# Six column chunks of the merge gates as seven-for-eight block products, moved behind the recurrent branch

## The chip, the cores and the metric

The kernel runs on one core of one Trainium2 chip. The metric is the device time in microseconds (us) of one execution, median of three runs. The engines are named as in the profile: PE multiplies matrices (PEld is its weight load), DVE, ACT and POOL work on tiles, SP issues most of the transfers.

## What is computed

One trunk layer of a streaming encoder, 512 frames by 1024 features, in float32. Cut to what the change touches:

```python
xn = rmsnorm(x, norm_mix_g)
q, k, v, xr, gr, ga, gb = split(xn @ w_in)      # seven parts of 1024 columns each
ya = chunked_band_attention(q, k, v) @ w_attn_out
xc = causal_depthwise_conv(xr)                  # four taps
r, i = sigmoid(block_diag(xc, w_rg_r) + b_r), sigmoid(block_diag(xc, w_rg_i) + b_i)
a = exp(-8 * r * softplus(-lam))
h = scan(a, sqrt(1 - a * a) * i * xc)           # h[t] = a[t] * h[t-1] + ...
yb = (h * gelu(gr)) @ w_rnn_out
out = x + (sigmoid(ga + b) * ya + sigmoid(gb + b) * yb) @ w_o   # then the feed-forward half
```

## The kernel before

**Products.** Every float32 operand is split into a high and a low part (ACT copies the high part, DVE subtracts it to leave the low one: `split`, lines 80 to 83), and every product is three matmuls (`mm3`, lines 74 to 78). A projection of `xn` goes by chunks of 256 columns: `project` makes two output tiles of 128 columns by 512 frames, each with 8 blocks of the contraction times 3 matmuls, so 48 matmuls of 512 frames a chunk. The feed-forward half makes ten pairs of its chunks in another way (`block_product`, line 360): a chunk is cut into 2 by 2 blocks of the weights and 2 by 2 blocks of the activations, and seven products of the blocks' sums stand for the eight products of the blocks. That is 7 times 4 times 3, or 84, matmuls of 256 frames. The sums of the weights' blocks are made by DVE for each chunk (`weight_sums`), those of the activations once.

**Room for weights.** A chunk's raw weights land in one of three `raw` tiles and are split into `whl` tiles, of which there are four, two to a chunk; the list `chunks` says in which order. `weights(name, ahead)` makes the chunk and the next `ahead` ones.

**The stage around the change.** After the norm comes the recurrent branch, in four pairs of feature tiles (j = 0, 2, 4, 6). A pair's work is:

- the chunk `xr`; then `rnn_conv`: ACT `conv_in` (L668), three DVE taps (L675), ACT L679 and POOL L680 split the result into `xch`;
- the chunk `gr`; then the GeLU: ACT L691, DVE L692, ACT L696, DVE L697. It makes a tile `g`, of which there are two, out of a PSUM bank `t`, of which there are two;
- `gates_of`: twelve small matmuls (`rg`, L709) read `xch`; then eight ACT gates (L721), two ACT tiles `u` (L728), two exponentials (L729), DVE L731, POOL L733, DVE L735, L736; one ACT square root for the pair (L759, with a table load before and one behind it); then for each tile `rnn_scan`: DVE L740, the scan L741, L742, which reads `g` for the last time, and ACT L746 and POOL L747 for the two parts of `rnn`;
- one or two chunks of the merge gates `ga`, `gb` with a `tanh` each (L780).

So the order on PE is xr0, gr0, ga0, rg(0), gb0, xr2, gr2, rg(2), ga2, gb2, xr4, gr4, rg(4), gb4, xr6, gr6, rg(6), gb6; then q and k of the first pair of heads, v, the recurrent branch's way out `yb` (contracting over all eight `rnn` tiles), and the attention. The chunks ga4 and ga6 come late in the attention.

**What sets the order.** Apart from marked stretches the order of each engine's instructions is made when the kernel is built, by a scheduler that takes whatever it holds to be ready, in general the earliest in the text first; an instruction far down in the text may so be placed early if its room and its inputs are free. `keep_in_program_order` puts an instruction behind everything of its engine that is ahead of it in the text. On the chip each engine then goes through its list in order.

Of the kernel before, what the change touches and what calls it, by code (L numbers as in the profile page):

```python
# [14 lines left out]
P = 128  # L15
D = 1024
S = 512
# [21 lines left out]
def block_kernel(ctx: ExitStack, tc: tile.TileContext, x, norm_mix_g, w_in, b_merge, rel_table,  # L39
# [31 lines left out]
    def mm_tile(name, tag="mm"):  # L71
        return ps.tile([P, S], F32, tag=tag, bufs=4 if tag == "mm" else 2, name=name)

    def mm3(o, sh, sl, mh, ml, start, stop, parts=False):

        pe.matmul(o, sh, mh, start=start, stop=False, skip_group_check=parts)  # L76
        pe.matmul(o, sh, ml, start=False, stop=False, skip_group_check=parts)  # L77
        pe.matmul(o, sl, mh, start=False, stop=stop, skip_group_check=parts)  # L78
# [14 lines left out]
    index = {}  # L93
    strassen = [f"f{w}{j}" for j in range(2, FT, 2) for w in "gu"]

# [14 lines left out]
    def plan_v(gr):  # L110
        plan(f"v{gr}", cols(w_in, C_V + gr * CW))

    plan_qk(0)
# [43 lines left out]
    def load(name, k):  # L157
        _, parts, rows, kts = chunks[index[name]]
        wide = sum(width for *_, width in parts)
        n = min(4 * CW // wide, kts - k)  # L160
        at = rows + k * P
        pl, bufs = wp, 3
        if name in strassen and name[0] == "f":
# [12 lines left out]
    room = [None]  # L176

    begun = {}
    spare = [None]

    def weight_sums(name, ahead=False):
# [8 lines left out]
        if name not in begun:  # L190
            a11, a21, a12, a22 = blocks_of()
            s21, s34 = (sums_room.tile([P, 2, 4, P], F32, tag=tag, bufs=1, name=f"{tag}_{name}")
                        for tag in ("s21", "s34"))
            s2, s1, s3, s4 = s21[:, 0], s21[:, 1], s34[:, 0], s34[:, 1]
            first_sum = dve.tensor_add(s1, a21, a22)
            if name == "fu2":

                tc.keep_in_program_order(first_sum)
            dve.tensor_sub(s2, s1, a11)
            dve.tensor_sub(s3, a11, a21)  # L200
            dve.tensor_sub(s4, a12, s2)
        if ahead:
            slots[0] += 1
            o = sums_room.tile([P, 2, 2, 4, P], F32R, tag="whl", bufs=1, name=f"whl_{name}_s2")
# [11 lines left out]
        for group in ((("a11", a11), ("a12", a12)), (("s2", s2), ("s1", s1)), (("s3", s3), ("s4", s4)), (("a22", a22),)):  # L216
# [10 lines left out]
            if len(group) == 2:  # L227
                slots[0] += 1
                pl, tag, bufs = (sums_room, "whl", 1) if slots[0] % 5 == 1 else (wp, "whl", 4)
            o = pl.tile([P, len(group), 2, 4, P], F32R, tag=tag, bufs=bufs, name=f"whl_{name}_{group[0][0]}")  # L230
# [236 lines left out]
    gm = cp.tile([P, 8], F32, name="gm")  # L467
    _, xnT = features(xnp, "xn", "xnT")

# [233 lines left out]

    def rnn_gate_products(j, xch, tag):

        pos = [ps.tile([P, S], F32, tag=tag, bufs=4 if tag == "mm" else 2, name=f"rg{j}_{n}") for n in range(2)]
        for n, (wp_, xp) in enumerate(((0, 0), (1, 0), (0, 1))):
            for po, rows in zip(pos, (slice(0, HD), slice(HD, P))):
                ins = pe.matmul(po[:], wrg[rows, wp_, j], xch[rows, xp], start=n == 0, stop=n == 2)  # L709
                if j == n == 0:  # L710

                    tc.keep_in_program_order(ins)
        return pos

# [39 lines left out]
    def gates_of(j):  # L754
        pos = [rnn_gate_products(j + c, conv[j + c][1], ("s", "mm")[c]) for c in range(2)]
        for c in range(2):
# [21 lines left out]
    def gate(w, j):  # L778
        po = tile_of(f"g{'ab'[w]}{j - j % 2}", j % 2, "t" if j < 2 and w == 0 else "mm")
        act.activation((ta, zB)[w][j], po[:], AF.Tanh, bias=hb[:, 16 + 8 * w + j:17 + 8 * w + j], scale=0.5)  # L780
# [4 lines left out]
    with tc.manual_schedule(engines={mybir.EngineType.Activation, mybir.EngineType.DVE}):  # L785
        po = [tile_of("xr0", c, ahead=0) for c in range(2)]
        xc = [conv_in(0, po[0])]
        conv_taps(0, po[0], xc[0])
        prefetch(index["ga0"] + 1)
        xc.append(conv_in(1, po[1]))  # L790
# [5 lines left out]
        g.append(gelu_in(1, po[1]))  # L796
        prefetch(index["gb0"] + 1)
        for c in range(2):
            gelu_out(g[c], po[c])
            conv[c] = xc[c], xch[c], g[c]  # L800
    for j in range(0, KT, 2):
        if j:
            for c in range(2):
                conv[j + c] = rnn_conv(j + c, tile_of(f"xr{j}", c, ahead=2))
        for c in range(2):
            if j:
                po = tile_of(f"gr{j}", c, "t")
                conv[j + c] += (rnn_gelu(j + c, po),)
        if j:
            gates_of(j)  # L810
        for w in range(j // 4, 2):
            for c in range(2):
                gate(w, j + c)
            if j == w == 0:
                gates_of(j)

# [43 lines left out]
    rw2_stack.close()  # L860
    rw_stack.close()
    aw2_stack, aw2 = opened("aw2", 2)
    aw_stack, aw = opened("aw", 2, "right")
# [140 lines left out]

    sums_room = ctx.enter_context(pool_of("sums", 1, "right"))
    hn_stack, hnp = opened("hnT", 1, "right")
# [111 lines left out]
    def split_act(i):  # L1118
        o = act2[i]

        if i == 0:
            hi = acp.tile([P, 2, S], F32R, tag="act", bufs=13, name=f"act_hi{i}")
        elif i < 3:
            hi = sums_room.tile([P, 2, S], F32R, tag=("s21", "s34")[i - 1], bufs=1, name=f"act_hi{i}")
        else:
            if i == 3:
                hi_room.append(sums_room.tile([P, 2, 2, S], F32R, tag="whl", bufs=1, name="act_hi34"))
            hi = hi_room[0][:, i - 3]
# [231 lines left out]
```

## Time and profile before

| what | value |
|---|---|
| median of 3 runs | 867.27 us (867.13 to 867.33) |
| the profiled execution: its own time, its span | 867.3 us, 865.5 us |
| DVE, ACT, POOL busy over the span | 600.9, 498.1, 95.2 us |
| rg(0), rg(2), rg(4), rg(6) start at | 47.5, 82.0, 127.4, 161.8 us |
| first and last matmul of `yb` start at | 191.0, 241.4 us |
| first block product of the feed-forward half starts at | 544.9 us |

The profiled execution is the time of the runs within 0.1 us, so sums made against its span are sums against the median; 1.8 us lie outside the span. A busy time of an engine adds up the intervals in which it had an instruction in work. Matmuls overlap in their pipe, so the time that one takes up on PE is read from the distance of two starts, not from its own duration.

### The profile page before, as it was taken

The page shows a single profiled execution, that of the slowest core. Times are in us where ns is not written, and L with a number is a line of the kernel's source. Part 1 is how long each engine was busy: PE and PEld are TensorE (multiplying, and loading weights), DVE is VectorE, ACT ScalarE, POOL GpSimd, SP SyncE. Part 2 cuts the span into 40 slices and gives each one's busy share as a digit, 9 for nine tenths or more (in the row PEclk, how much of TensorE's full clock was granted, in tenths as well). Part 3 has the DMA queues.
Part 4 walks back from the last instruction along what each step waited for, and adds up shares of the span by engine and source line. Part 5 has one row for each costly group of instructions (what it writes and reads, how often), then busy time and mean ns, then how long its engine had stood idle before and what let it go on. Part 6 is the DMA issues. An engine that isn't in the chain of part 4 may idle for free.

```text
span 865.5 us, 13353 instructions
## 1 busy us (share of the span) xinstructions
PE 856.4 (99%) x5130; PEld 761.1 (88%) x5130; DVE 600.9 (69%) x950; ACT 498.1 (58%) x878; POOL 95.2 (11%) x161
## 2 busy tenths in 40 slices
PE   9999999999999999999999999999999999999997
PEld 6988888888889889898888889999999999888885
DVE  5666656573456585766556556988888888698885
ACT  6595747752356585767633357555555556545434
POOL 2412111120112132221200000000000001000000
PEclk9999999999999999999999999999999999999999
DMA  9133232433323332232223712424333332437542
GB/s 289 57 119 106 68 120 76 123 98 98 109 88 95 81 103 74 81 113 64 74 76 121 266 51 72 145 79 131 109 98 98 99 98 85 148 100 227 185 134 97
DMA packets 88767, 96.39 MB, mean 111 GB/s; under 512 B 5784, under 2 KB 74992, under 8 KB 88704
## 3 DMA queue, kind: packets, MB, share of 16 engines
q1 hardware_dynamic: 87072, 92.03, 34.3%
q10 hardware_dynamic: 1232, 2.95, 0.9%
q8 instruction: 40, 0.66, 0.3%
q0 software_dynamic: 400, 0.57, 0.2%
q14 instruction: 23, 0.19, 0.1%
HBM read 93.39 MB, written 2.14 MB: 110 GB/s over the span
## 4 chain that ended last, share of the span: by engine, by line
PE 97%; DVE 1%; ACT 1%; DMA 0%; issue 0%; ACTq 0%; DVEq 0%
PE po_out L76 2%; PE po_out L77 2%; PE po_out L78 2%; PE o L941 2%; PE p_fu L78 2%; PE p_fg L78 2%; PE p_fg L77 2%; PE p_fg L76 2%; PE p_fu L76 2%; PE p_fu L77 2%; PE pT L921 2%; PE po_v L76 2%; PE po_v L78 2%; PE po_v L77 2%; PE po_gb L76 2%; PE po_xr L77 2%
## 5 line engine op out<-in xcount | busy, mean ns | idle before, releaser
L910 POOL TENSOR_SCALAR p<-p,rl 128x128 f32<-128x128 f32 (+3 forms) x61 | 34.9, 590 | 135.7 <-DVE rl L906 135.4
L905 ACT ACTIVATE p<-p,m 128x128 f32<-128x128 f32 (+1 forms) x64 | 35.7, 560 | 11.0 <-DVE m L904 10.8
L76 PE MATMUL po_v<-whl_v,xnT 128*128 128x256 f32 x128 | 36.5, 285 | 0.0
L78 PE MATMUL po_v<-whl_v,xnT 128*128 128x256 f32 x128 | 36.2, 283 | 0.0
L77 PE MATMUL po_v<-whl_v,xnT 128*128 128x256 f32 x128 | 36.2, 283 | 0.0
L1131 POOL TENSOR_TENSOR act_lo<-act,act_hi 128x1024 fp32r<-128x1024 f32 x1 | 2.4, 2405 | 300.7 <-ACT act_hi L1130 300.7
L76 PE MATMUL po_out<-whl_fo,act_hi 128*128 128x512 f32 (+1 forms) x80 | 30.8, 385 | 0.5 <-ACT c_u L370 0.5
L78 PE MATMUL po_out<-whl_fo,act_lo 128*128 128x512 f32 (+1 forms) x80 | 30.7, 384 | 0.0
L77 PE MATMUL po_out<-whl_fo,act_hi 128*128 128x512 f32 (+1 forms) x80 | 30.7, 384 | 0.0
L904 DVE CUSTOM_DVE_ANT_0 p<-s,bias 128x128 f32<-128x128 f32 (+1 forms) x64 | 29.1, 483 | 1.0 <-PE s L896 1.0
L83 DVE TENSOR_TENSOR whl_qk<-raw_qk,whl_qk 128x1024 fp32r<-128x1024 f32 x16 | 20.5, 1284 | 13.2 <-ACT whl_qk L82 13.0
L83 DVE TENSOR_TENSOR whl_fu_s<-s_fu,whl_fu_s 128x1024 fp32r<-128x1024 f32 x20 | 24.1, 1222 | 6.2 <-ACT whl_fu_s L82 6.2
L77 PE MATMUL po_xr<-xnT,whl_xr 128*128 128x512 f32 (+1 forms) x80 | 27.7, 353 | 0.0
L83 DVE TENSOR_TENSOR pp<-pT,pp 128x384 fp32r<-128x384 f32 (+1 forms) x48 | 27.5, 596 | 0.1
L77 PE MATMUL po_gr<-xnT,whl_gr 128*128 128x512 f32 (+1 forms) x80 | 27.5, 347 | 0.0
L78 PE MATMUL po_gr<-xnT,whl_gr 128*128 128x512 f32 (+1 forms) x80 | 27.3, 347 | 0.0
L78 PE MATMUL po_xr<-xnT,whl_xr 128*128 128x512 f32 (+1 forms) x80 | 27.2, 346 | 0.0
L76 PE MATMUL po_gr<-xnT,whl_gr 128*128 128x512 f32 (+1 forms) x80 | 27.2, 347 | 0.0
L83 DVE TENSOR_TENSOR whl_fg_s<-s_fg,whl_fg_s 128x1024 fp32r<-128x1024 f32 x20 | 24.0, 1222 | 4.1 <-ACT whl_fg_s L82 4.0
L76 PE MATMUL po_xr<-xnT,whl_xr 128*128 128x512 f32 (+1 forms) x80 | 26.3, 351 | 0.4 <-ACT xnT L566 0.4
L82 ACT ACTIVATE whl_qk<-raw_qk 128x1024 fp32r<-128x1024 f32 x16 | 16.8, 1053 | 17.0 <-PE po_yb L78 10.4
L76 PE MATMUL po_gb<-xnT,whl_gb 128*128 128x512 f32 x64 | 25.2, 394 | 0.0
(487 smaller groups left out, 3247.5 us busy)
## 6 DMA issues: line engine op xcount, KB each, us to landing
raw_fg<-in_w_ffn_in_dram SPq DMA_DIRECT2D x24, 512.0 KB, 4.2
raw_fu<-in_w_ffn_in_dram SPq DMA_DIRECT2D x22, 512.0 KB, 3.9
raw_qk<-in_w_in_dram SPq DMA_DIRECT2D x32, 256.0 KB, 3.2
raw_fo<-in_w_ffn_out_dram SPq DMA_DIRECT2D x16, 512.0 KB, 3.6
raw_xr<-in_w_in_dram SPq DMA_DIRECT2D x8, 512.0 KB, 4.3
raw_gr<-in_w_in_dram SPq DMA_DIRECT2D x8, 512.0 KB, 3.6
raw_ga<-in_w_in_dram SPq DMA_DIRECT2D x8, 512.0 KB, 4.7
raw_gb<-in_w_in_dram SPq DMA_DIRECT2D x8, 512.0 KB, 3.5
```

What stands on the lines that cost most here:

```text
L76: pe.matmul(o, sh, mh, start=start, stop=False, skip_group_check=parts)
L77: pe.matmul(o, sh, ml, start=False, stop=False, skip_group_check=parts)
L78: pe.matmul(o, sl, mh, start=False, stop=stop, skip_group_check=parts)
L82: act.activation(hi, src, AF.Copy)
L83: dve.tensor_sub(lo, src, f(hi))
L904: dve.tensor_tensor_reduce(prob[qb][:], scs[qb][:, 0:w], bias[:, S - w:S], -1.0, 3e38, ALU.add, ALU.min, nmax[:, qb:qb + 1])
L905: act.activation(prob[qb][:], prob[qb][:], AF.Exp, bias=nmax[:, qb:qb + 1], scale=-1.0, accum_out=lsum[:, qb:qb + 1])
L910: eng.tensor_scalar(prob[qb][:], prob[qb][:], rl[:, qb:qb + 1], 1.0, ALU.mult, ALU.mult)
L921: pe.transpose(pt[:, at * P:(at + 1) * P], prob[qb][:, kb * P:(kb + 1) * P], ident[:])
L941: pe.matmul(po[:, S - n:S], st, pp[i][:, part, lo:lo + n], start=kb == 0 and part == 0, stop=kb == NT - 1 and part == 1)
L1131: (dve if i else pool).tensor_sub(lo[:], o[:], f(hi[:]))
```

## The change

The chunks ga0, ga2, gb0, gb2, gb4 and gb6 leave the recurrent branch. The branch keeps xr, gr and the gates of each pair; the gates of pair 0 come between xr2 and gr2. The twelve small matmuls of a pair are put in another order (the low part of `xch` last), and the first of them and the first matmul behind them are kept in program order. Behind q and k of the first heads a new pool `gs` is opened where the branch's pool `rw` was closed: its first tiles hold the high and low parts of four sums of blocks of `xn`, and behind them lies room for sums and raw weights. Then come yb0, yb2, yb4, gb0, yb6, gb2, gb4, gb6, ga0 and ga2, the six gates as block products, and after them the scores of the first head and v. `yb` is now copied out by ACT, and DVE multiplies it with the gate when that is there.

```diff
+    behind = []
     def mm3(o, sh, sl, mh, ml, start, stop, parts=False):
-        pe.matmul(o, sh, mh, start=start, stop=False, skip_group_check=parts)
+        ins = pe.matmul(o, sh, mh, start=start, stop=False, skip_group_check=parts)
+        if behind:
+            tc.keep_in_program_order(ins)
+            behind.clear()
...
-    strassen = [f"f{w}{j}" for j in range(2, FT, 2) for w in "gu"]
+    strassen = ["gb0", "gb2", "gb4", "gb6", "ga0", "ga2"] + [f"f{w}{j}" for j in range(2, FT, 2) for w in "gu"]
...
-        if j < 4:
-            plan(f"ga{j}", cols(w_in, C_GA + j * P))
-        plan(f"gb{j}", cols(w_in, C_GB + j * P))
...
     plan_qk(0)
+    for j in (0, 2, 4):
+        plan_yb(j)
+    for j in range(0, KT, 2):
+        plan(f"gb{j}", cols(w_in, C_GB + j * P))
+        if j == 0:
+            plan_yb(6)
+    for j in (0, 2):
+        plan(f"ga{j}", cols(w_in, C_GA + j * P))
     plan_v(0)
-    for j in range(0, KT, 2):
-        plan(f"yb{j}", cols(w_rnn_out, j * P))
...
-    def rnn_gate_products(j, xch, tag):
+    def rnn_gate_products(j):
+        pos = [[ps.tile([P, S], F32, tag=tag, bufs=4 if tag == "mm" else 2, name=f"rg{j + c}_{n}") for n in range(2)]
+               for c, tag in enumerate(("s", "mm"))]
+        behind.append(j)
+        for c, wp_, xp in ((0, 0, 0), (0, 1, 0), (1, 0, 0), (1, 1, 0), (0, 0, 1), (1, 0, 1)):
+            for po, rows in zip(pos[c], (slice(0, HD), slice(HD, P))):
+                ins = pe.matmul(po[:], wrg[rows, wp_, j + c], conv[j + c][1][rows, xp], start=wp_ == xp == 0, stop=xp == 1)
+                if behind:
+                    tc.keep_in_program_order(ins)
+                    behind.clear()
+        behind.append(j)
+        return pos
...
+    for j in range(2, KT, 2):
         for c in range(2):
+            conv[j + c] = rnn_conv(j + c, tile_of(f"xr{j}", c, ahead=2))
+        if j == 2:
+            gates_of(0)
+        for c in range(2):
+            po = tile_of(f"gr{j}", c, "t")
+            conv[j + c] += (rnn_gelu(j + c, po),)
+        gates_of(j)
...
+    gs_stack, gs = opened("gs")
+    bt_homes = {i: gs.tile([P, 2, 4, 256], F32R, name=f"xt{i}") for i in (2, 1, 3, 4)}
+    sums_room[0] = room[0] = gs
+    def way_out(j):
+        for c in range(2):
+            po = mm_tile(f"po_yb{j + c}")
+            project(po, weights(f"yb{j}"), c, rnn)
+            act.activation(zB[j + c], po[:], AF.Copy)
...
+    def sums_of_x():
+        x32 = gs.tile([P, 2, 4, 256], F32, tag="whl", name="x32")
+        x12, x22 = x32[:, 0], x32[:, 1]
...
+        dve.tensor_add(x12, f(block_of_x(0, 1, 0)), f(block_of_x(0, 1, 1)))
+        dve.tensor_sub(t1[:], x12, f(block_of_x(0, 0, 0)))
...
+        for i, t in ((2, t2), (1, t1), (3, t3), (4, t4)):
+            split_pair(bt_homes[i], t[:])
...
+    def block_gate(w, j, n, x_right):
+        z = zs[0][j // 2] if w == 0 else zs[0][2 + n % 2]
+        block_product(f"g{'ab'[w]}{j}", n % 2, x_right, z[:].rearrange("p a (b n) -> p (a b) n", n=256))
+        for c in range(2):
+            at = 16 + 8 * w + j + c
+            act.activation(z[:, c], z[:, c], AF.Tanh, bias=hb[:, at:at + 1], scale=0.5)
+        if w:
+            o = zs[1][j // 2]
+            dve.scalar_tensor_tensor(o[:], z[:], 1.0, o[:], ALU.add, ALU.mult)
+    way_out(0)
+    x_right = sums_of_x()
+    for j in (2, 4):
+        way_out(j)
+    for n, (w, j) in enumerate(((1, 0), (1, 2), (1, 4), (1, 6), (0, 0), (0, 2))):
+        block_gate(w, j, n, x_right)
+        if n == 0:
+            way_out(6)
+    gs_stack.close()
...
+    prob = scores(0)
     for t in range(NT):
         v_tile(0, t)
-    for j in range(KT):
-        if j == 6:
-            prob = scores(0)
-        po = mm_tile(f"po_yb{j}")
-        project(po, weights(f"yb{j - j % 2}"), j % 2, rnn)
-        dve.scalar_tensor_tensor(zB[j], zB[j], 1.0, po[:], ALU.add, ALU.mult)
```

In `sums_of_x` eight DVE instructions over 1024 elements make the four sums out of `xn`, which is there from the start of the branch, and four ACT and four DVE instructions split them.

More of the change, by code (lines that the diff above doesn't have):

```diff
@@ L162, in load @@
         pl, bufs = wp, 3
-        if name in strassen and name[0] == "f":
+        if name in strassen:
             loads[0] += 1
@@ L467, in block_kernel @@
     gm = cp.tile([P, 8], F32, name="gm")
-    _, xnT = features(xnp, "xn", "xnT")
+    xnT_all, xnT = features(xnp, "xn", "xnT")
     vc = cp.tile([P, NV], F32, name="vc")
@@ L702, in rnn_gelu @@
         return g
-    def rnn_gate_products(j, xch, tag):
[L706 to L710, printed above, removed]
+    def rnn_gate_products(j):
[6 more added lines that the diff above has]
+                if behind:
                     tc.keep_in_program_order(ins)
+                    behind.clear()
+        behind.append(j)
         return pos
@@ L754, in gates_of @@
     def gates_of(j):
-        pos = [rnn_gate_products(j + c, conv[j + c][1], ("s", "mm")[c]) for c in range(2)]
+        pos = rnn_gate_products(j)
         for c in range(2):
@@ L778, in gate @@
     def gate(w, j):
-        po = tile_of(f"g{'ab'[w]}{j - j % 2}", j % 2, "t" if j < 2 and w == 0 else "mm")
+        po = tile_of(f"g{'ab'[w]}{j - j % 2}", j % 2)
         act.activation((ta, zB)[w][j], po[:], AF.Tanh, bias=hb[:, 16 + 8 * w + j:17 + 8 * w + j], scale=0.5)
@@ L788, in block_kernel @@
         conv_taps(0, po[0], xc[0])
-        prefetch(index["ga0"] + 1)
+        prefetch(index["xr2"] + 1)
         xc.append(conv_in(1, po[1]))
@@ L796, in block_kernel @@
         g.append(gelu_in(1, po[1]))
-        prefetch(index["gb0"] + 1)
+        prefetch(index["gr2"] + 1)
         for c in range(2):
@@ L861, in block_kernel, with block_of_x @@
     rw_stack.close()
+    gs_stack, gs = opened("gs")
[6 more added lines that the diff above has]
+            act.activation(zB[j + c], po[:], AF.Copy)
+    def block_of_x(kh, half, part):
+        return xnT_all[:, 4 * kh:4 * kh + 4, part, half * 256:half * 256 + 256]
+    def sums_of_x():
+        x32 = gs.tile([P, 2, 4, 256], F32, tag="whl", name="x32")
+        x12, x22 = x32[:, 0], x32[:, 1]
+        t1, t2, t3, t4 = (gs.tile([P, 4, 256], F32, tag=tag, bufs=bufs, name=f"x_t{i + 1}")
+                          for i, (tag, bufs) in enumerate((("s21", 1), ("s34", 1), ("a22", 2), ("a22", 2))))
+        dve.tensor_add(x12, f(block_of_x(0, 1, 0)), f(block_of_x(0, 1, 1)))
+        dve.tensor_sub(t1[:], x12, f(block_of_x(0, 0, 0)))
+        dve.tensor_sub(t1[:], t1[:], f(block_of_x(0, 0, 1)))
+        dve.tensor_add(x22, f(block_of_x(1, 1, 0)), f(block_of_x(1, 1, 1)))
+        dve.tensor_sub(t2[:], x22, t1[:])
+        dve.tensor_sub(t3[:], x22, x12)
+        dve.tensor_sub(t4[:], f(block_of_x(1, 0, 0)), t2[:])
+        dve.tensor_add(t4[:], t4[:], f(block_of_x(1, 0, 1)))
+        for i, t in ((2, t2), (1, t1), (3, t3), (4, t4)):
+            split_pair(bt_homes[i], t[:])
+        return right_side(lambda kh, half, part, k: block_of_x(kh, half, part)[:, k], [bt_homes[i] for i in range(1, 5)])
+    def block_gate(w, j, n, x_right):
[16 more added lines that the diff above has]
+    gs_stack.close()
     aw2_stack, aw2 = opened("aw2", 2)
@@ L1003, in block_kernel @@
     hp = ctx.enter_context(pool_of("h", 1, "right"))
-    sums_room = ctx.enter_context(pool_of("sums", 1, "right"))
+    sums_room[0] = ctx.enter_context(pool_of("sums", 1, "right"))
+    slots[0] = loads[0] = 0
     hn_stack, hnp = opened("hnT", 1, "right")
```

27 lines of the change are left out of this document (8 added, 19 removed).

## The prediction

> **What bounds the kernel now.** I read the page first, then the list of who waited for whom, then the order of time around the branch.
>
> ```profile
> PE 856.4 (99%) x5130; PEld 761.1 (88%) x5130; DVE 600.9 (69%) x950; ACT 498.1 (58%) x878; POOL 95.2 (11%) x161
> ...
> PEclk9999999999999999999999999999999999999999
> ...
> PE 97%; DVE 1%; ACT 1%; DMA 0%; issue 0%; ACTq 0%; DVEq 0%
> ```
>
> PE is in work for 99% of the span, at full clock in every slice, and it is 97% of the chain that ended last. The longest of PE's waits is at the very start:
>
> ```profile
> PE busy L396 <- DVE eps_t L402: 1.2, 1, 1.2
> ```
>
> So the kernel is as long as its matmuls, and there are two ways for a change to move it: fewer or shorter matmuls, or a wait where none is. The shares of DVE (69%) and ACT (58%) are means over the whole kernel; they don't say whether there is slack in the branch that the change squeezes. That comes below.
>
> **What PE saves.** A matmul's time on PE is the distance of two starts:
>
> ```profile
> 60.12 0.39 PE L76 MATMUL po_xr<-xnT,whl_xr 128*128 128x512 f32 x1
> ...
> 71.00 0.39 PE L76 MATMUL po_gr<-xnT,whl_gr 128*128 128x512 f32 x1
> ```
>
> ```profile
> 569.95 0.28 PE L76 MATMUL p_fu<-bt,whl_fu_a 128*128 128x256 f32 x1
> ...
> 570.43 0.28 PE L77 MATMUL p_fu<-bt,whl_fu_a 128*128 128x256 f32 x1
> ```
>
> The whole chunk xr2, 48 matmuls of 512 frames, takes 71.00 - 60.12 = 10.88 us, 0.2267 each. The block products of the feed-forward half step by 0.48 us in four, 0.120 each, so 84 take 10.08. Halving the frames does not halve the time: from 0.2267 = 2w + c and 0.120 = w + c, w is 0.107 and c is 0.0133 us a matmul, and 84 short ones pay c more often than 48 long ones. A chunk saves 0.80 us, six save **4.8 us**. That is all that the change can win on PE; the small matmuls `rg` are the same twelve in another order, `yb`, q, k and v the same matmuls elsewhere.
>
> [...]
>
> **What the branch loses: its cover.** The gates stood between the pairs as pure PE work while ACT and DVE did a pair's long chain. I take the stretch from rg(0) to rg(6).
>
> ```profile
> 47.60:161.80 114.20, 114.20 (x518) 92.98 (x518) 74.12 (x86) 78.28 (x102) 22.10 (x18) 1.00 0.32 98
> ```
>
> Columns: length; PE, PEld, DVE, ACT, POOL busy. In it go, by tile (for the tanhs the columns are DVE, ACT; for the weights PE, PEld, DVE, ACT; the rows are za, zb, whl_ga, whl_gb):
>
> ```profile
> 47.60:161.80 114.20, 0.00 (x0) 2.04 (x3) 1.00 0.32 98
> 47.60:161.80 114.20, 0.00 (x0) 4.10 (x6) 1.00 0.32 98
> 47.60:161.80 114.20, 11.17 (x48) 8.93 (x48) 2.88 (x2) 2.09 (x2) 1.00 0.32 98
> 47.60:161.80 114.20, 33.39 (x144) 26.88 (x144) 8.74 (x6) 6.31 (x6) 1.00 0.32 98
> ```
>
> PE: the four chunks gb0, ga2, gb2, gb4 leave it, and xr2 moves ahead of rg(0) into the place of ga0: 114.2 - 5 x 10.88 = 59.8 us are left. ACT: 78.28 - 2.04 - 4.10 - 2.09 - 6.31 = 63.7. The splits of xr and gr in the stretch become eight:
>
> ```profile
> L82 ACT ACTIVATE whl_gr<-raw_gr 128x1024 fp32r<-128x1024 f32 x6 | 6.3, 1050 | 0.0
> L82 ACT ACTIVATE whl_xr<-raw_xr 128x1024 fp32r<-128x1024 f32 x5 | 5.3, 1053 | 1.1 <-PE po_gr L78 0.7 <-DMA raw_xr<-in_w_in_dram 0.3
> ...
> L82 ACT ACTIVATE whl_qk<-raw_qk 128x1024 fp32r<-128x1024 f32 x1 | 1.0, 1046 | 0.0
> ```
>
> Three fewer of eleven, and both of qk0 in place of one: two fewer, 2.1 us. **ACT has 61.7 us of work for 59.8 us of PE.** DVE: 74.12 - 2.88 - 8.74, less three of its splits (1.3 each), is 58.6 us, also nearly all of it. In the profile of before the same work had 114 us. The branch stops being bound by PE.
>
> How full can these engines get? Other stretches of this trace:
>
> ```profile
> 49.10:71.00 21.90, 21.90 (x99) 18.13 (x97) 14.18 (x17) 18.56 (x24) 4.95 (x4) 1.00 0.36 114
> 161.80:174.40 12.60, 12.60 (x62) 10.17 (x62) 6.74 (x10) 11.88 (x17) 1.50 (x4) 1.00 0.42 127
> ```
>
> ACT is busy for 18.56 of 21.9 us (85%) behind rg(0) and for 11.88 of 12.6 (94%) behind rg(6). At 94% the 61.7 us last 65.6, at 85% 72.6: PE waits 5.8 to 12.8 us. From the other side the wait may be nothing: not all is due before rg(6), see the first rival. I take 92%, near the fuller row since the scheduler has more to fill gaps with: 67.1 us, **7.3 us of waits**.
>
> **Where the first wait falls.** gr4 writes PSUM banks `t`, and these are held by the GeLU of pair 2, which needs a tile `g` that L742 of pair 0 must have read.
>
> ```profile
> 47.52 1.66 PE L709 MATMUL rg<-xch,wrg 64*128 64x512 f32 x12
> ```
> ```profile
> 65.69 0.67 DVE L742 SCALAR_TENSOR_TENSOR u<-u,g 128x512 f32<-128x512 f32 x1
> ```
> ```profile
> L691 ACT ACTIVATE g<-po_gr x8: 578/592/601, 36.8 to 161.9; 128x512 f32<-128x512 f32 x8
> L692 DVE SCALAR_TENSOR_TENSOR g<-g,po_gr x8: 679/688/689, 41.6 to 162.5; 128x512 f32<-128x512 f32 x8
> L696 ACT ACTIVATE g<-g x8: 618/632/634, 44.7 to 166.1; 128x512 f32<-128x512 f32 x8
> L697 DVE SCALAR_TENSOR_TENSOR g<-g,po_gr x8: 680/686/689, 46.2 to 166.8; 128x512 f32<-128x512 f32 x8
> ```
>
> rg(0) stays at 47.5. Behind its 1.6 us come gr2, rg(2) and xr4, so PE wants gr4 at 49.1 + 10.9 + 1.6 + 10.9 = 72.5. L742 ended at 66.4 in the profile of before; now the conv of pair 2 runs in the same stretch:
>
> ```profile
> L675 DVE SCALAR_TENSOR_TENSOR xc<-po_xr,vc,xc x24: 735/748/752, 33.8 to 156.4; 128x511 f32<-128x511 f32 x8, 128x510 f32<-128x510 f32 x8, 128x509 f32<-128x509 f32 x8
> L668 ACT ACTIVATE xc<-po_xr,vc x8: 758/766/782, 33.0 to 152.7; 128x512 f32<-128x512 f32 x8
> L679 ACT ACTIVATE xch<-xc x8: 614/632/634, 36.2 to 157.3; 128x512 fp32r<-128x512 f32 x8
> ```
>
> That is 2 x (0.77 + 0.63) = 2.8 us on ACT for the two tanhs (1.4) that go, and 6 x 0.75 = 4.5 on DVE, so L742 ends 1.4 to 5 us later, at 67.8 to 71.4. The GeLU adds 0.59 + 0.69 + 0.63 + 0.69 = 2.6, and each of the four waits for about half of an instruction that runs (2 us in all): 72.4 to 76. A wait at gr4 of 0 to 3.5 us, and it holds back everything behind gr4 in PE's list, rg(4) and the pinned xr6 among it. The rest of the 7.3 comes at rg(4), xr6 and rg(6), from the balance above.
>
> **Behind the branch.** `yb0` needs all eight `rnn`:
>
> ```profile
> 183.53 2.55 POOL L747 TENSOR_TENSOR rnn<-u,rnn 128x512 fp32r<-128x512 f32 x2 [8.71 <-ACT rnn L746]
> ```
>
> The last is there 186.1 - 161.8 = 24.3 us after rg(6) starts. Now q and k cover 1.6 + 10.9, and the first six of eight blocks of each `yb` tile 4.1 more; two such tiles can be begun, two more if their weights are split. 12.5 + 8.2 to 16.4 against 24.3: nothing, to 3.6 us; it is within the 5.8 to 12.8. The sums of blocks cost DVE 1.22 us an instruction:
>
> ```profile
> L83 DVE TENSOR_TENSOR whl_fu_s<-s_fu,whl_fu_s 128x1024 fp32r<-128x1024 f32 x20 | 24.1, 1222 | 6.2 <-ACT whl_fu_s L82 6.2
> ...
> 542.00:742.00 200.00, 200.00 (x1669) 200.00 (x1668) 165.18 (x225) 117.34 (x208) 2.40 (x1) 1.00 0.34 105
> ```
>
> Twelve take 14.7 us, under yb0, yb2 and yb4 (32.6 us). The second row is the feed-forward half, 20 block products: DVE 8.3 us in each 10.08; a gate adds 0.6 (its 1.22 us product for half of one), ACT two tanhs, 1.4, to 5.9. Both fit, so the six products run without waits, as they do there. If that cover were gone, DVE at 8.9 would still be under 10.08. SP issues the same loads, later; in the branch four of them in 23.4 us, as dense as before (0.32 of the queues). The first head's scores:
>
> ```profile
> 229.43 0.22 PE L895 MATMUL s<-kh,q 128*128 128x128 f32 x1
> ```
> ```profile
> 234.69 2.06 POOL L910 TENSOR_SCALAR p<-p,rl 128x128 f32<-128x128 f32 x4 [44.19 <-DVE rl L906]
> ```
>
> 7.3 us from score to scaled row; v behind it takes 4 x 24 x 0.12 = 11.5 on PE. Nothing.
>
> **The sum.** 867.3 - 4.8 + 7.3 = **869.8 us**, slower by 0.3%.
>
> **The rivals.**
> 1. *The branch keeps up* (0.27). Of pair 4's work on ACT the two `u`, two exponentials, the root with its table loads and the `rnn` copies, about 8 us, are due only at yb0 and can slide behind rg(6). Then ACT needs 53.6 of 59.8 us, 90%, less than the fuller row above. For it: list order lets late work slide. Against it: the tiles `g` tie L742 of pair 4 to the GeLU of pair 6, and what slides lengthens the 24.3 us. It decides at waits under 3.1 us; with none 862.5, with 3.1 865.5: faster.
> 2. *The waits eat the gain* (0.20): 3.1 to 6.5 us, 865.6 to 869.0, no measurable change.
> 3. *The sums of x don't stay behind the branch* (0.08): they need only `xn` and their room lies behind the branch's. The scheduler takes work early where it can:
>
> ```profile
> 168.60 0.15 POOL L655 MEMSET bias<- 64x64 f32 x1 [9.27 <-DMA bias<-ext_d]
> ```
>
> This belongs to the first head's scores (229.4), 61 us later. Then DVE has 58.6 + 8 x 1.22 = 68.4 us in the stretch, at 92% 74.3: waits of 14.5, 877.0.
> 4. *The clock falls after a long wait* (0.05). No trace of mine shows a fall: the clock row is full throughout, and no wait is over 1.2 us. A price is bounded by nothing and by one chunk at half pace, 10.9; half of that gives 875.2. [...]
>
> **How the numbers follow.** The forecast has 0.40, with 869.0 to 875.3 of its own (waits 6.5 to 12.8). A measurement of this kernel tells 0.2%, 1.7 us, from no change. Rival 1 is faster (0.27), rival 2 the same (0.20), the rest slower (0.53). From 862.5 (no wait) to 875.3 (85%) holds all but rivals 3 and part of 4.
>
> **What would show it.** PE's list of waits gets entries at gr4 (some 3 us), rg(4), xr6 or rg(6), where the list of before has one of 1.2; ACT and DVE are over 90% busy between rg(2) and rg(6); block gates step by 0.120. Wrong if rg(6) starts near 107 (47.5 + 59.8) and nothing waits, or if the waits lie at the block products.

## The result and the profile after

The changed kernel takes **882.6 us** (882.24 to 883.14, four runs) where the kernel before takes 867.3 beside it: a ratio of 1.0177, interval 1.016 to 1.0195. It is 15.3 us slower, outside the range of 862.5 to 875.3. Line numbers from here on are those of the changed kernel (`rg` L724, conv L680 and L687, `xch` L691 and L692, gates L737, `ti * xc` L752, scan L757, `rnn` L762 and L763). The first lines of its page: engines, clock row, chain.

```profile
PE 857.0 (97%) x5346; PEld 768.4 (87%) x5346; DVE 647.7 (74%) x1012; ACT 524.4 (60%) x938; POOL 97.9 (11%) x161
...
PEclk9998999999999999999999999999999999999999
...
PE 83%; DVE 7%; ACT 6%; issue 1%; DMA 1%; POOL 1%; ACTq 0%; DVEq 0%; POOLq 0%
```

PE has fallen from 97% to 83% of the chain that ended last, and one slice of the clock row is no longer full. The span is 880.5 us, 15.0 longer. Who PE waited for (us in total, times, longest):

```profile
PE rg L724 <- ACT xch L691: 6.4, 3, 3.6
PE rg L724 <- POOL xch L692: 2.7, 4, 0.9
PE po_yb L78 <- ACT rnn L762: 1.3, 1, 1.3
...
PE po_yb L82 <- POOL rnn L763: 1.1, 2, 0.6
PE pT L984 <- DVE v L88: 0.9, 1, 0.9
PE po_v L78 <- DVE v L88: 0.6, 1, 0.6
```

Where before nothing above 1.2 us stood, `rg` now waits 9.1 us for the conv, `yb` 2.7 with one small entry more, v and the first transposes 1.5. The first wait, in PE's order of time (start, us, and in brackets the idle time ahead):

```profile
60.36 0.73 PE L724 MATMUL rg<-xch,wrg 64*128 64x512 f32 x4
61.91 0.50 PE L724 MATMUL rg<-xch,wrg 64*128 64x512 f32 x2 [0.82 <-POOL xch L692]
66.00 1.22 PE L724 MATMUL rg<-xch,wrg 64*128 64x512 f32 x4 [3.60 <-ACT xch L691]
67.77 0.79 PE L724 MATMUL rg<-xch,wrg 64*128 64x512 f32 x2 [0.55 <-POOL xch L692]
68.50 0.79 PE L78 MATMUL po_xr<-xnT,whl_xr 128*128 128x512 f32 x1
69.09 0.63 PE L82 MATMUL po_xr<-xnT,whl_xr 128*128 128x512 f32 x1
69.51 0.63 PE L83 MATMUL po_xr<-xnT,whl_xr 128*128 128x512 f32 x1
...
72.44 0.39 PE L78 MATMUL po_xr<-xnT,whl_xr 128*128 128x512 f32 x1
```

Behind the wait of 3.60 us the matmuls of xr4 step by 0.42 to 0.43 us in place of 0.227, until 72.4. The same stretch in one row (length; PE, PEld, DVE, ACT, POOL busy; granted clock):

```profile
66.00:72.10 6.10, 5.55 (x15) 3.62 (x16) 6.02 (x7) 6.00 (x7) 1.64 (x1) 0.50 0.50 153
```

Half the clock for 6.1 us with 5.55 in work: 2.8 us more.

**The account.** The six chunks save 4.8, so 19.8 us are lost against that. From the starts of the groups, with 10.88 us for a chunk and 1.8 for a free `rg` (before, ten chunks and three `rg` make the 114.2 us from rg(0) to rg(6)): rg(2) starts at 60.36 and rg(4) at 92.25, 31.9 us for 1.8 + 21.8, 8.3 lost; rg(4) to rg(6) (117.56) 1.7; rg(6) to the first gate product (170.22) 52.7 us for 1.8 + 10.9 + 32.6, 7.4. The rest, 2.4, lies behind, 1.5 of it in the waits of v and the first transposes. Nothing is lost in the block products, which step as predicted:

```profile
170.22 0.28 PE L78 MATMUL p_gb<-xnT,whl_gb_a 128*128 128x256 f32 x1
...
171.53 0.28 PE L83 MATMUL p_gb<-xnT,whl_gb_a 128*128 128x256 f32 x1
```

Eleven steps in 1.31 us, 0.119 each.

**Why pair 2's conv is late.** In the text it comes ahead of the gates of pair 0. ACT and DVE in order of time:

```profile
49.52 5.60 ACT L737 ACTIVATE gt<-rg,hb 64x512 f32<-64x512 f32 x8
55.15 0.82 ACT L744 ACTIVATE u<-gt,sp 128x512 f32<-128x512 f32 x1
55.87 0.76 ACT L680 ACTIVATE xc<-po_xr,vc 128x512 f32<-128x512 f32 x1
```

```profile
52.33 0.69 DVE L752 SCALAR_TENSOR_TENSOR gt<-gt,xc 128x512 f32<-128x512 f32 x1 [1.46 <-ACT gt L737]
55.21 0.69 DVE L752 SCALAR_TENSOR_TENSOR gt<-gt,xc 128x512 f32<-128x512 f32 x1 [2.19 <-ACT gt L737]
```

There are two tiles `xc`; pair 0 holds them until L752 has read them, and L752 needs the gates, which need rg(0). So the conv starts at 55.9, though xr2 was done when rg(0) began at 47.7. The first tile is free at 53.0, but by its list ACT is in its eight gates until 55.1. That is one held tile, and a list that was made with it. Is it the cause?

The whole branch, from rg(0) to the last `rnn`, and what ACT and DVE waited for in it:

```profile
47.70:117.56 69.86, 63.70 (x277) 49.40 (x276) 55.31 (x68) 56.92 (x76) 17.30 (x15) 0.95 0.28 84
47.70:153.10 105.40, 93.58 (x407) 72.03 (x406) 84.01 (x99) 82.08 (x111) 31.10 (x24) 0.97 0.27 82
```

```profile
ACT xch L691 <- DVE xc L687: 7.8, 3, 6.2
ACT rnn L762 <- DVE u L758: 5.7, 3, 2.8
ACT kh L864 <- DVE kl L863: 3.1, 1, 3.1
```

```profile
DVE gt L752 <- ACT gt L737: 10.9, 6, 2.2
DVE u L747 <- ACT gt L745: 3.1, 2, 1.6
DVE g L709 <- ACT g L708: 2.7, 2, 2.1
```

Each engine is in work for about 80% of 105 us. Over all entries of these lists 17.1 of ACT's 23.3 idle us are waits for DVE, and 20.9 of DVE's 21.4 are waits for ACT. The largest other one is a wait of ACT for a transfer of weights, 2.0 us at rg(0).

### The profile page after: what moved, and what is told of

Its sections match the earlier page's. It is cut to its first block, busy times and chain, and to the rows that moved or that the text cites. A ratio compares the mean times of both kernels' runs of the same rounds, so it can differ in the third digit from the quotient of the medians.

```text
span 880.5 us, 13925 instructions
## 1 busy us (share of the span) xinstructions
PE 857.0 (97%) x5346; PEld 768.4 (87%) x5346; DVE 647.7 (74%) x1012; ACT 524.4 (60%) x938; POOL 97.9 (11%) x161
## 4 chain that ended last, share of the span: by engine, by line
PE 83%; DVE 7%; ACT 6%; issue 1%; DMA 1%; POOL 1%; ACTq 0%; DVEq 0%; POOLq 0%
PE po_out L78 2%; ACT gt L737 2%; PE po_out L83 2%; PE po_out L82 2%; PE o L1004 2%; PE p_fu L83 2%; PE p_fg L83 2%; PE p_fg L82 2%; PE p_fg L78 2%; PE p_fu L78 2%; PE p_fu L82 2%; PE pT L984 2%; PE po_h L83 2%; PE po_ya L83 2%; PE po_h L82 2%; PE po_ya L78 2%
## 5 line engine op out<-in xcount | busy, mean ns | idle before, releaser
L968 ACT ACTIVATE p<-p,m 128x128 f32<-128x128 f32 (+1 forms) x64 | 35.7, 560 | 12.8 <-DVE m L967 12.4
L83 PE MATMUL po_out<-whl_fo,act_lo 128*128 128x512 f32 (+1 forms) x80 | 30.7, 384 | 0.0
L82 PE MATMUL po_out<-whl_fo,act_hi 128*128 128x512 f32 (+1 forms) x80 | 30.7, 384 | 0.0
L82 PE MATMUL po_xr<-xnT,whl_xr 128*128 128x512 f32 (+1 forms) x80 | 28.4, 362 | 0.0
L83 PE MATMUL po_xr<-xnT,whl_xr 128*128 128x512 f32 (+1 forms) x80 | 27.9, 355 | 0.3 <-DVE whl_xr L88 0.3
L78 PE MATMUL po_xr<-xnT,whl_xr 128*128 128x512 f32 (+1 forms) x80 | 27.4, 365 | 0.4 <-ACT xnT L578 0.4
L83 PE MATMUL po_gr<-xnT,whl_gr 128*128 128x512 f32 (+1 forms) x80 | 27.3, 347 | 0.0
L78 PE MATMUL po_gr<-xnT,whl_gr 128*128 128x512 f32 (+1 forms) x80 | 27.3, 348 | 0.0
L78 PE MATMUL po_yb<-rnn,whl_yb 128*128 128x512 f32 x64 | 24.7, 394 | 1.7 <-ACT rnn L762 1.3
L82 PE MATMUL po_yb<-rnn,whl_yb 128*128 128x512 f32 x64 | 25.2, 393 | 1.1 <-POOL rnn L763 1.1
```

Source lines behind the costliest of these rows:

```text
L78: ins = pe.matmul(o, sh, mh, start=start, stop=False, skip_group_check=parts)
L968: act.activation(prob[qb][:], prob[qb][:], AF.Exp, bias=nmax[:, qb:qb + 1], scale=-1.0, accum_out=lsum[:, qb:qb + 1])
```

## The experiments

Three theories, by letters in what follows. **A**: a tile is held too long (xc, then another). **B**, the one of the prediction, called the load theory in later expectations: ACT and DVE have that much work. **D**: the two work through ordered lists and stand waiting for each other, so that the work takes a quarter longer than its sum. They were judged by time, by PE's waits and by the start of the last `rnn` (the last POOL instruction that writes it). "Loss" is the profiled span less what PE's work alone would give, 865.5 - 0.8 for each block product.

| version | time, us | last `rnn` starts | block products | loss |
|---|---|---|---|---|
| changed kernel | 882.6 | 150.8 | 6 | 19.8 |
| e1, e5, e10: more buffers | 880.8, 879.65, 877.98 | 149.1, 148.1, 147.0 | 6 | 18.4, 17.1, 16.0 |
| e2: plain products behind | 885.25 | 150.7 | 0 | 17.8 |
| e6, e7, e8: less work | 879.03, 881.06, 879.08 | 147.4, 147.6, 145.5 | 6 | 16.5, 18.0, 16.5 |
| e14, e15: conv to `rg` cut | 883.12, 880.13 | 153.5, 148.6 | 6 | 20.8, 18.0 |
| e17, e18: gate links cut | 873.06, 873.0 | 134.2, 133.8 | 6 | 10.5, 11.2 |
| e3, e4: one, three covers | 878.76, 870.82 | 158.5, 169.3 | 5, 3 | 15.6, 5.9 |
| e9, e13, e20: three, and v | 878.22, 867.61, 866.36 | 170.2, 170.2, 166.6 | 3 | 13.5, 2.9, 1.5 |
| e19: two, and v | 869.99 | 160.4 | 4 | 5.9 |

### More buffers (e1, e5, e10)

```diff
-        xc = rw.tile([P, S], F32, tag="xc", name=f"xc{j}")
+        xc = rw.tile([P, S], F32, tag="xc", bufs=4, name=f"xc{j}")
```

> The changed kernel with four buffers of the tile xc in place of two, nothing else; 882.6 us without it. Theory A (a chain): the conv of pair 2 could not start until the gates of pair 0 had read their two xc, which held the first wait, 5.0 us at rg(2), and the half clock behind it. With four buffers that wait falls under 1.5 us, the clock row is full, and the time falls by 5 to 8.5 us, to 874 to 877.6. Rival B (a balance): ACT and DVE have some 62 and 59 us of work for 60 us of TensorE from rg(0) to rg(6), whatever the order; then the waits of that stretch stay 7 to 8 us in sum, later or spread, and only the 2.8 us of half clock may go: 879.5 to 882.6.

880.8 us. B's size, and the reason shows in PE's waits of this version:

```profile
PE po_gr L78 <- DVE g L709: 7.5, 1, 7.5
PE rg L724 <- POOL xch L692: 2.0, 1, 2.0
PE rg L724 <- ACT xch L691: 1.8, 1, 1.8
```

rg(2) waits no more, and gr4 waits for the GeLU of pair 2: the place that the prediction named. e5 gives `g` four buffers as well, e10 `gt` and `a` too (`bufs=4` each).

> The changed kernel with four buffers of xc and four of g; with xc alone 880.8 us, where the wait moved from rg(2) to gr4 (7.5 us, until the GeLU of pair 2 had freed its PSUM bank, which itself waited for a tile g of pair 0). Theory A (the wait is a chain of buffers): with g free too, the GeLU of pair 2 runs as soon as gr2 is there, the wait at gr4 goes, and the time falls to 872 to 875. Rival B (ACT and DVE are behind by so much work, and a wait that is opened turns up at the next tile): the waits keep their sum, at rg(4), xr6 or rg(6): 878.5 to 881.5.

> The changed kernel with four buffers of each tile of the branch: xc, g, both gt and a; with xc and g alone 879.65 us. Theory A in its last form (some tile of pair j is still held when pair j + 2 wants it): no tile is left to wait for, waits fall to 2 to 4 us, 868 to 873. Theory D (two engines that work in turns, in the order of their lists): nothing is held by a tile any more and the waits stay, 878 to 880.5.

879.65 and 877.98 us: now rg(4) waits 5.5 and 4.8 in all, rg(6) 3.2 and 3.1. With four of each of these tiles (`xch`, `u` and the PSUM banks keep their number) the time is 4.6 us shorter, against a loss of 19.8. In all three versions the clock falls twice, for 6.8 us each time, the second time at rg(6), where it did not fall in the changed kernel. At the granted 0.50 that second fall hides at most 3.4 us more of gain, an estimate from the 6.8 us; even so A explains less than half. A falls as the main cause; a held tile in the main chose the place of the wait.

### The place alone (e2)

```diff
-    x_right = sums_of_x()
...
-        block_product(f"g{'ab'[w]}{j}", n % 2, x_right, z[:].rearrange("p a (b n) -> p (a b) n", n=256))
...
+            po = tile_of(f"g{'ab'[w]}{j}", c)
```

> The changed kernel with its six gates as plain products at the same places behind the branch, and without the sums of blocks of x; 882.6 us without it. If the block products run free and the whole loss is that of the place, the six chunks cost 6 x 0.80 = 4.8 us more: 887.4, within 1 us, and every wait before yb0 is what it was. Rival C (the sums cost time too): twelve instructions of DVE and four of ACT for the sums of x stand beside the last pair's scans and hold up yb; without them the 4.1 us lost at yb shrink, and the time is 883.3 to 886.

885.25 us: slower than the changed kernel, but by 2.65 in place of 4.8. Rival C of this expectation has the size, but its reason doesn't show: of the waits at `yb` 0.4 is left here, but only since yb0 starts 2.3 us later (136.0 for 133.7) while the last `rnn` starts as late as there (150.7). What makes yb0 late is a second fall of the clock, at rg(6), for 6.8 us (120.45 to 127.28). So the block products bring 2.65 us at least, and whether the other 2.15 are the price of the sums stays open. The move alone costs 885.25 - 867.06 = 18.2 us.

### Less work (e6, e7, e8)

```diff
-        act.activation(u_pairs[-1][:], u_pairs[-1][:], AF.Sqrt, scale=-1.0)
+        act.activation(u_pairs[-1][:], u_pairs[-1][:], AF.Tanh, scale=-1.0)
...
-        for d in range(1, 4):
+        for d in range(1, 4 if j < 2 else 2):
```

The first pair of lines is e6, which leaves the square root out, the second e7, which leaves out two taps; both together are e8.

> The changed kernel with Tanh in the place of the square root of each pair: the root of 1 - a^2 is left out of what is computed, its instruction keeps its size, and ACT loads no table between the pairs, 2 x 1.28 us less for each, 7.7 us up to rg(6). Rival B with ACT as the engine that is behind: the waits up to rg(6) fall by most of that, time 873 to 876. With DVE as the one that is behind: 880 to 882.6. Theory A (buffers hold conv(2) until the gates of pair 0 are done, at 55.9): the first table load lies behind rg(2), so the first wait at rg(2) stays 3 to 5 us with its half clock; 877 to 880.

> The changed kernel with one of three taps of the conv for the pairs 2, 4 and 6: two taps are left out of what is computed, 12 instructions of 0.75 us on DVE, 9 us up to rg(6), and each pair's conv is 1.5 us shorter for each of its two tiles. Rival B with DVE as the engine that is behind: the waits fall by most of 9 us, 872 to 875. With ACT as the one that is behind, only the shorter way from xr to rg tells, some 2 to 4 us: 878 to 880. Theory A: the start of conv(2) stays at 55.9, its end comes 2 to 3 us sooner, the half clock goes: 876 to 878.

> The changed kernel with both reliefs at once: Tanh in place of the root (the root left out, no table loads between pairs) and one of three taps for pairs 2, 4 and 6 (two taps left out). Alone they gave 3.6 and 1.5 us, though each took 8 to 9 us of work from its engine. Theory D (ACT and DVE work in turns on one pair at a time, so relief of one engine only moves the wait to where the other is behind): together they give more than their sum, all waits up to rg(6) but 2 us go, and the time falls to 866 to 870. If the reliefs only add (each cut shortens a few waits by itself): 877 to 878.

879.03, 881.06 and 879.08 us. Ten us less of ACT gained 3.6, nine less of DVE 1.5, and both together no more than the root alone. e6 lies in the range that theory A gave it (877 to 880), and rg(2) still waits 3.6 us there, as A said; e7 lies 3 us above A's. Theory D's forecast for e8 (866 to 870) missed as widely as the load theory's for e7. e8's branch, to its last `rnn`:

```profile
47.70:147.70 100.00, 91.38 (x397) 71.86 (x397) 75.21 (x86) 72.45 (x104) 33.34 (x24) 0.95 0.25 80
```

DVE has 8.8 us less to do than in the changed kernel, ACT 9.6, and the branch is 5.4 shorter: the engines are 75% and 72% full. What was taken out came back as idle time; ACT waits 12.4 us for DVE L758 alone, where it waited 5.7.

### Links cut (e14, e15, e17, e18)

```diff
-                ins = pe.matmul(po[:], wrg[rows, wp_, j + c], conv[j + c][1][rows, xp], start=wp_ == xp == 0, stop=xp == 1)
+                ins = pe.matmul(po[:], wrg[rows, wp_, j + c], xch_0[c][rows, xp], start=wp_ == xp == 0, stop=xp == 1)
```

> The changed kernel, but the recurrent gate products of pairs 2, 4 and 6 read the conv of pair 0 (the conv of the other pairs is computed and not used there), so that no rg waits for a conv; every instruction stays, on every engine. Load theory (ACT and DVE have too much work for the stretch): no engine has less to do, so the waits turn up at gr4, xr6 and yb0, 877 to 881. Chain theory (the way from xr over conv to rg and from there over the gates back to the tiles of the next pair is too long for two chunks of TensorE): the link from conv to rg is cut, the waits at rg go and nothing takes their place but 2 to 4 us at yb0: 866 to 871.

> The same cut, with four buffers of xc and g too, so that neither the conv nor a held tile stands between the pairs; all instructions stay. Load theory: 877 to 881 again, the wait at yb0 above all. Chain theory: 865 to 869, and if the cut alone left a wait at gr4 (the GeLU of pair 2 waits for a tile g of pair 0), it is gone here.

883.12 us, 2 above the load theory's range, and 880.13, inside it; the chain theory's ranges (866 to 871, 865 to 869) are far off. In e15 no `rg` waits, and the waits stand elsewhere:

```profile
PE po_k L78 <- ACT g L708: 3.3, 1, 3.3
PE po_yb L78 <- ACT gt L737: 1.8, 1, 1.8
PE po_yb L78 <- ACT kh L866: 1.6, 1, 1.6
PE po_yb L78 <- ACT rnn L762: 1.3, 1, 1.3
```

So PE can be let free at any place; it meets the branch again at the next, `yb` at the latest. What counts is when ACT and DVE are through. e17 leaves them all their instructions and takes away that they wait for each other inside the gates:

```diff
-        dve.scalar_tensor_tensor(u, tr[:], 1.0, u, ALU.add, ALU.mult)
+        dve.scalar_tensor_tensor(us[:], pos[0][:], 1.0, k0[:, 0], ALU.add, ALU.mult)
...
-        dve.scalar_tensor_tensor(ti[:], ti[:], 1.0, xc[:], ALU.add, ALU.mult)
+        dve.scalar_tensor_tensor(ts[:], pos[1][:], 1.0, k0[:, 0], ALU.add, ALU.mult)
```

> The changed kernel with the links between ACT and DVE inside the gates cut, and all instructions kept in size and number: DVE's six steps of a gate work on tiles of their own from the gate products and a tile of zeros, ACT's tanhs, exponentials, roots and rnn copies on theirs (the recurrence is not computed from the gates). Conv, GeLU and weight splits keep their links. Load theory (some 80 us of work on each engine until the last rnn is what takes 103 us): 877 to 881, as with every other version without cover. Theory D (ACT and DVE are in order and wait for one another; in the changed kernel ACT's idle time of 21 us there is mostly a wait for DVE and DVE's mostly a wait for ACT): both run over 90% full, the last rnn is there some 12 us sooner, and the waits that are left are 2 to 5 us: 866 to 870.

873.06 us, 9.5 less: the first version without cover that comes out well under 878. It lies between the two forecasts, 4 us under the load theory's and 3 above D's. The last `rnn` in the changed kernel, in e15 and in e17 (POOL; the first and the last start stand behind the durations), and e17's branch:

```profile
L763 POOL TENSOR_TENSOR rnn<-u,rnn x8: 1277/1395/2274, 75.4 to 150.8; 128x512 fp32r<-128x512 f32 x8
```
```profile
L763 POOL TENSOR_TENSOR rnn<-u,rnn x8: 1277/1392/2280, 75.7 to 148.6; 128x512 fp32r<-128x512 f32 x8
```
```profile
L767 POOL TENSOR_TENSOR rnn<-u,rnn x8: 1283/1838/2277, 67.2 to 134.2; 128x512 fp32r<-128x512 f32 x8
```
```profile
47.70:136.20 88.50, 84.49 (x375) 66.55 (x374) 76.30 (x97) 79.91 (x109) 28.58 (x23) 0.96 0.30 91
```

Nearly the same work on ACT (79.9 us for 82.1) now takes 88.5 us in place of 105.4: ACT is 90% full, DVE 86%. DVE's sum is 7.7 less: 3.5 of it are the first sums of x, which come behind the stretch here, some 3 the gate steps, shorter on tiles of their own (`ti * xc` 0.69 us on average for 0.82), and the rest is in the main one split of weights fewer. Where the time is won shows when the stretch is cut at rg(6), first the changed kernel behind it, then e17 ahead of it and behind it:

```profile
117.56:153.10 35.54, 29.88 (x131) 22.63 (x130) 28.69 (x32) 25.17 (x35) 13.81 (x9) 1.00 0.24 77
```
```profile
48.85:114.81 65.96, 62.98 (x278) 49.66 (x278) 57.59 (x73) 58.69 (x80) 23.81 (x18) 0.95 0.29 89
114.81:136.20 21.39, 20.37 (x94) 16.21 (x94) 17.56 (x22) 20.58 (x29) 4.77 (x6) 1.00 0.26 85
```

Ahead of rg(6) e17 takes 66.0 us for 69.9, with ACT 89% full for 81%; behind it 21.4 for 35.5, with ACT 96% full for 71%. So 14 of the 17 us are won behind rg(6), where the last pair's gates and what has slid behind it are left. e17 also frees xc and `g` sooner; e10 shows what that brings by itself, 4.6 of the 9.5 us and 4 of the 17 at the last `rnn`.

> Both cuts at once: the links between ACT and DVE inside the gates, and the link from conv to the gate products of pairs 2, 4 and 6 (the recurrence is not computed); every instruction stays. With the first alone 873.06 us, where a wait of 2.9 us at rg(4) for the conv and the slow clock behind it were left; with the second alone 883.1. Theory D (mutual waits): the two have the same root, so that now no wait over 1.5 us is left before yb0, and the time is 866 to 869, near the 865.5 that the TensorE gain and no wait but those of v and the first transposes (3 us) give. Load theory (the second cut alone gained nothing, so it gains nothing here either): 872 to 875.

873.0 us: e18 adds the cut of e14, with fewer buffers of the gate tiles than e17 has (`us` 3 for 4, `ts` and `a` 2 for 3). It lies in the load theory's range. No `rg` waits, and the 2.9 us of rg(4) and the slow clock of e17 (0.88 and 0.90 on average over 75 to 92 and 92 to 107 us) come back as 2.8 and 4.1 us at `yb`, with the last `rnn` at 133.8. D in its strict form (no loss left) is refuted: with most of the mutual waits gone, the 80 us of work still cost PE 6.9 us of waits at `yb`. B in its strict form is refuted by e17.

### Cover put back (e3, e4, e9, e13, e19, e20)

e4 leaves ga0, ga2, gb6 plain behind rg(0), rg(2), rg(4); e3 only ga0; e19 ga0 and gb6.

```diff
         gates_of(j)
+        cover(cover_gr.get(j))
```

> One gate, ga0, goes back as plain products behind rg(0), ahead of gr2; five block products stay. It costs 0.8 us of TensorE. Theory A: pair 2's conv is in time, so the 5.0 us at rg(2) and 2.8 us of half clock go, and the 1.9 at rg(4), 3.4 at rg(6) and 4.1 at yb stay: 875 to 876. Rival B: the 10.9 us of cover bring only 2.1 us of work on ACT and two tanhs, 1.4, and 2.5 on DVE, so that some 7 of the 7.8 us of waits up to rg(6) go wherever they were: 873 to 874.

> Three gates stay plain as cover, ga0 behind rg(0), ga2 behind rg(2), gb6 behind rg(4); three block products behind the branch (gb0, gb2, gb4), worth 2.4 us. Both theories: no wait at any rg. Then what is left of the loss is that at yb (4.1 us) and ahead of the first transposes (1.5): 867.3 - 2.4 + 5.6 = 870.5 if these have nothing to do with the backlog of the branch, 865 to 867 if they are its tail (ACT and DVE behind at rg(6)) and go with it.

878.76 and 870.82 us. e3 is 3 us slower than either theory said: its wait went from rg(2) to rg(4) (4.05 us, and the slow clock again, 0.50 until 107.6), so one chunk of 10.88 us bought 4.2 us. Three take every wait at `rg` away; what stays, at `yb` and at the first transposes, is the 870.5 of the expectation.

e9 puts v ahead of `yb` (a small room of its own for four of its tiles), e13 also moves yb6 behind the first head's scores:

```diff
+    for t in range(NT):
+        v_tile(0, t)
     way_out(0)
...
     prob = scores(0)
+    way_out(6)
```

> The version with three plain gates as cover (870.8 us, three block products, 2.4 us less of TensorE) with the first group of v ahead of yb0 in place of behind the block products, as in the kernel before. What was lost there lies at yb (2.2 us beyond the kernel before), v (0.5) and the first transposes (0.9 and what follows it). If v's 11.5 us cover the last pair's work: 867.0 to 868.3, the same as the kernel before. If the splits that v brings (two of weights, four of results, some 5 us on ACT and 6 on DVE) delay the last pair by as much as they cover: 870 to 871.

> Three plain gates as cover and v ahead of yb0 (878.2 us), with yb6 moved behind the first head's scores. There the first transposes waited 6.1 us for the scaled rows of the scores, with a slow clock behind it; v had been their cover. If yb6's 10.9 us of TensorE cover the 7.3 us from score to row, both go: 867 to 868.5, the same as the kernel before. If the scores start late for another reason (their room opens only when the block products are done), 2 to 4 us of wait stay: 870 to 873.

e9: 878.22. The wait for `rnn` at `yb` went (0.85 is left, for weights), and a new one came, since v had been the cover of the first softmax:

```profile
PE pT L1010 <- POOL p L999: 6.3, 2, 6.1
```

e13 gives that place another cover, and the time is 867.61, ratio 1.0006 (0.9997 to 1.0016): what the expectation had, and no different from the kernel before.

> Two plain gates as cover, ga0 behind rg(0) and gb6 behind rg(2); four block products (3.2 us less of TensorE); v ahead of yb0, yb6 behind the scores, four buffers of xc and g. From rg(0) to where yb0 needs the last rnn TensorE has some 80 us of work, 21.8 of cover and 11.5 of v, 114; ACT and DVE took 103 us in the changed kernel and get some 12 more to do with two gates and v. If they stay within that, the waits are under 2 us: 865.5 to 867.0, the first that is faster than the kernel before. If a wait at rg(4) or rg(6), ahead of v, opens the clock's fall: 868 to 873.

> Three plain gates as cover, v ahead of yb0, yb6 behind the scores (867.61 us), with four buffers of xc and g. That version has 2.4 us less of TensorE and 2.9 us of small losses (0.8 of them a wait of yb for its weights). With more buffers the lists of ACT and DVE have more freedom: 866.5 to 867.3 if the wait for the weights goes; 867.6 if nothing changes.

e19: 869.99, in the second range, but not for its reason, since the clock doesn't fall in it (0.999 over the span). A wait of 1.5 at `yb` for its weights and 0.8 at `rg` are among its 5.9 us of loss; e13 loses 2.9, and the fourth block product saves 0.8. e20, four buffers of xc and `g` in e13: **866.36 us**, ratio 0.9991 (0.9982 to 1.0000); 0.14 under its range; no wait in the branch or at `yb` is left in its list. That is the best version found, 0.08% under the kernel before, at the edge of what can be told.

## Why the prediction was wrong, point by point

- **PE saves 4.8 us**: right. The block products step by 0.119 and wait for nothing; as a whole, by e2, 2.65 at least.
- **The balance, and the step that failed.** "At 92% fill 67.1 us, 7.3 us of waits." The amount was about right: 61.7 and 58.6 us were forecast up to rg(6), and 56.9 and 55.3 were done there, the rest a little later. The term that was mis-sized is the **fill**: about 80%, not 92%. The 94% came from a stretch behind rg(6) where ACT's work stood ready; in the squeezed branch each engine's next instruction is often the other's result. Over the whole branch the sum shows it. PE has 4 x 1.8 + 54.4 + 10.9 = 72.5 us of work from rg(0) to yb0 and did 12.2 of `yb` before it stood still: 85. The work is 82 us on ACT, and no more on DVE, whose 84 hold 3.5 us of sums of x. At 92% that is 89 us and a loss of 4, less than the forecast; measured are 105.4 us and 20, of which the account finds 17.4 (PE did a few more matmuls of `yb` between its waits). By place, 10.0 us are lost up to the start of rg(6) and 2.9 in its waits, where 7.3 were forecast, and 6.9 behind it, where the sum had nothing: the balance ended at rg(6), but the work goes on to the last `rnn`. e17, with most mutual waits cut, shows the fill moving to 90% on ACT and the loss to 10.5. e8 shows that the work alone doesn't set it.
- **yb0, "nothing, to 3.6 us; within the 5.8 to 12.8"**: 2.7 us of waits, the bottom of a loss of 4. The size held, but it came on top. The last `rnn` came 35.5 us after rg(6) began, not 24.3, a number from a trace in which nobody hurried ACT and DVE.
- **The first wait at gr4 (0 to 3.5 us)**: wrong place. The chain was read rightly (e1 brought it out, with 7.5 us), but one link ahead of it was missed: xc has two buffers as well, and their last reader needs the gates of the pair before.
- **The clock, rival 4 (0.05)**: happened, for 2.8 us, with 0.50 granted for 6.8 us; the sum had it at nothing. That a fall would go to half pace was the author's estimate, which no row of before shows.
- **The sums of x, rival 3 (0.08)**: they stayed behind the branch. The first of them starts when the last `rnn` (150.8) is about to:

```profile
L892 DVE TENSOR_TENSOR x<-xnT x1: 2299/2299/2299, 149.6 to 149.6; 128x1024 f32<-128x1024 f32 x1
```

- **Scores and v at nothing**: 1.5 us of waits, and e9 shows how near the edge that stood.
- **The direction** (0.53 for slower) held; the signs named came true but for gr4. ACT and DVE over 90% between rg(2) and rg(6): no, 79% and 85%, and this was the step in another form.

What stays open: how much of the 20% is the order of the lists and how much the dependences themselves; a branch ordered by hand was not tried.

## What to carry to other kernels

A share of busy time in a stretch that nobody waits for says little about how full the engines get when they become the bound. If two engines pass a tile to and fro, count the idle time that each spends waiting for the other; in this kernel it was a fifth, and removing work from one or both moved it, not the end. Work on PE that "covers" such a chain can be moved only where other cover stands, and each cover taken has to be followed to the next place that waits (here conv, GeLU, `yb`, first softmax).

## What the runs showed of the hardware

**Half clock came in lengths of 3.41 us.** In the traces of all runs every stretch of half clock between the kernel's start and its end lasts 3.41 us or two or three times that: 6.83 in the changed kernel, from 65.51 to 72.33, three times 3.41 at the first fall of e6, once in e15 and e18. The ends of the two stretches lie 27.3 us apart in e3 and 30.7 in e5, eight and nine such lengths. The length of one wait did not decide here: at rg(6) the clock fell in e3 behind waits of 0.97 and 0.88 us and stayed up in the changed kernel behind waits of 2.05 and 0.88. How long PE was in work within one such length, in the changed kernel (with the first half of its fall behind it), e2, e3, and the changed kernel at rg(6) (window; PE busy first, the clock third from the end):

```profile
62.10:65.51 3.41, 0.30 (x2) 0.00 (x0) 3.41 (x6) 2.92 (x5) 0.78 (x1) 1.00 0.07 9
65.51:68.92 3.41, 2.37 (x7) 1.21 (x8) 3.33 (x3) 3.36 (x4) 1.64 (x1) 0.50 0.76 219
```
```profile
117.04:120.45 3.41, 1.47 (x9) 0.63 (x7) 3.41 (x5) 0.59 (x1) 0.00 (x0) 1.00 0.00 0
```
```profile
128.07:131.48 3.41, 1.56 (x10) 0.65 (x8) 2.90 (x4) 2.89 (x5) 2.13 (x2) 1.00 0.01 2
```
```profile
116.71:120.13 3.42, 1.82 (x11) 0.91 (x9) 3.42 (x5) 0.23 (x1) 0.00 (x0) 1.00 0.00 1
```

The windows from 62.10, from 117.04 (e2) and from 128.07 (e3), with 0.30, 1.47 and 1.56 us of work, were followed by half clock; the one from 116.71, with 1.82, was not. In e6 the clock fell behind windows with 1.8 and 2.0 us of work (read from the order of time; over 1.2 of it the small `rg` matmuls), so these rows show no amount of work that decides. What does stays open.

The price was 2.8 us in the changed kernel (the row of 66.00 to 72.10: 5.55 us of work at 0.50, half of which full clock would have saved); the half clock lasted two such lengths there.
